# One layer pair on one core: a gate moved ahead, table terms written straight to DRAM, a norm split 320/192 with ScalarE's root

## The chip, the cores and the metric

The kernel runs on one core of a Trainium2 chip. The metric is the device time of one execution in microseconds; the number that counts is the median of the runs. Engines are named as the profile names them: PE (TensorE matmuls), PEld (its weight loads), DVE (VectorE), ACT (ScalarE), POOL (GpSimd), SP (the queue that issues DMAs).

## The reference

512 tokens of width 1024 go through two blocks. The first is a convolution and a dilated attention side by side, then a feed-forward part; the second is a hybrid layer:

```python
proj = h @ w_in                                   # h: rms norm of x, modulated
xa, za, q, k, v, zb, qi, ki, wi, ga, gb = jnp.split(proj, IN_SPLITS, axis=-1)
ya = jax.nn.gelu(s5_mixer(xa, a_re, a_im, b_re, b_im, c_re, c_im, d_skip, log_dt))
g = ya @ w_glu + b_glu
ya = g[..., :SSM_WIDTH] * jax.nn.sigmoid(g[..., SSM_WIDTH:])
ya = (ya * jax.nn.silu(za)) @ w_a_o
yb = dsa_mixer(q, k, v, qi, ki, wi)               # attention over selected keys
yb = (yb * jax.nn.silu(zb)) @ w_b_o
merged = jax.nn.sigmoid(ga) * ya + jax.nn.sigmoid(gb) * yb
x = x + gate * (merged @ w_out)
return rms_norm_2(x, final_g)                     # x * rsqrt(mean(x*x) + 1e-6) * g
```

In the first block `mix = concat(rms_norm(y_conv), rms_norm(y_attn))` and `x + mix @ w_out`.

## The kernel before

Everything is held with channels on the 128 partitions and tokens (512) along the free axis. A product with a weight matrix runs in blocks of 128 output channels; weights and operands are split into a high and a low part (`wh`, `wl` and `hh`, `hl` and the like), so each block takes three matmuls for each 128 input channels: 24 matmuls for 1024, all into one accumulator (`steps`, L193 to L195). A weight tile comes in by DMA (`raw`, three buffers), ACT casts it to `wh` (L97) and DVE subtracts `wl` (L98).

The order on PE is made by interleaving: attention is written as the main line, and a generator (`self.filler`) is stepped between its parts to put projection matmuls in its gaps. `high_priority` lets the scheduler draw an instruction forward.

- **mix_out** (L544) multiplies the normed output of the convolution, later of the attention, by its half of `w_out`, eight columns of 128 outputs. Each column runs four input blocks. The sum of squares `sq` is turned into the root `r` behind column 0, and spread over the partitions by matmuls (`spread`) behind column 2. In the convolution the fourth input block (`ch`, `cl`, L504) is finished last.
- **ssm_tables** (L821 on) builds, between the gate and up products of the feed-forward part, three tables in DRAM (`tabs`) for the state space part: `tabs[0]` (`bts`, by PE transposes L933 and the ACT copy L934), `tabs[1]` (direct terms `kk`, PE L940, copied by ACT L943 and put into a block-triangular tile `tt` that POOL has cleared, by eight small DMAs inside the core, L954, and then one DMA to DRAM, L955) and `tabs[2]` (`ca`). `tt` and `bts` share one buffer (tag "io"). It is a generator, stepped between the feed-forward units. `nr` is a tile of its own.
- **gates** (L1237) is the filler of the second block's attention: eight projections for `szb` and `sza`, then eight gate projections with Tanh (`tanhs`), and the four output chunks of the state space part (`chunk_out`, L1194). A chunk copies the states `hs` (POOL), loads `cat` and `tt` from `tabs` (L1202, L1204) and runs eight pairs of matmuls (L1208, L1209). `cat` and `tt` of all chunks share two buffers, so a chunk's loads are issued when the chunk before has read both. Six gates come first, then chunk 0, gate 6, chunk 1, gate 7, chunk 2, chunk 3.
- **The last norm**: output blocks 5 to 7 of the last product run as two halves of 256 tokens, all three of the first half (`last(n, 0)`) and then those of the second. `norm(e)` sums the squares of a half by ones matmuls (L1383, L1386), takes the diagonal (L225, L228), makes the root by integer guess and three Newton steps on DVE (`rsqrt`, L204 to L212), spreads it (L236), and DVE multiplies the eight blocks (L1397), with an output DMA for each two. The first half's norm is interleaved with `last(6, 1)` and `last(7, 1)`.
- **WARM** fp32 matmuls on a tile of ones (L67) run at the start.

## Time and profile before

| | |
|---|---|
| median of three runs | 1020.39 us (1019.31 to 1023.40) |
| the profiled execution | 1019.43 us |
| its span in the trace | 1017.6 us (1.8 us lie around it) |
| mean granted clock of PE | 0.994 |
| PE busy | 992.5 us, 98% |
| DVE, ACT, POOL busy | 687.6, 420.7, 145.2 us |
| DMA moved | 125.12 MB, mean 123 GB/s |

Times in the rows are from the start of the span. PE's share is an average over all stages; a matmul's duration includes its way through the array, so what one costs in a stream is read from start to start. An idle time in brackets, with an arrow, names what the engine waited for last.

### The profile page before, as it was taken

To read this page: it belongs to the slowest core of one execution; us is meant where nothing else is said; L and a number is where in the kernel's file an instruction comes from. 1 tells how busy PE (TensorE), PEld (TensorE's weight loads), DVE (VectorE), ACT (ScalarE), POOL (GpSimd) and SP (SyncE) were. 2 spreads that over 40 slices of the span, in tenths; PEclk is the share of its full clock that TensorE was granted. 3 is DMA by queue.
4 is the path that set the end of the run, shared out by engine and by line. 5 is a ranking of instruction groups with operands and counts; after the bars stand their busy time and mean duration, and the time that the engine had idled before them with its cause. 6 is when DMAs were issued, how large, how long until landed. Compare 5 with 4: busy or idle time off the path is not lost.

```text
span 1017.6 us, 13862 instructions
## 1 busy us (share of the span) xinstructions
PE 992.5 (98%) x5074; PEld 824.4 (81%) x5074; DVE 687.6 (68%) x1334; ACT 420.7 (41%) x710; POOL 145.2 (14%) x324
## 2 busy tenths in 40 slices
PE   9999999999999999999999999999999979999995
PEld 7888887887777778888888898788888878888885
DVE  6886778786997847787653238599995555544444
ACT  6455556443333333233222225556445553333251
POOL 0000000007711100000010100001888130000020
PEclk9999999999999999999999999999999999999998
DMA  7343221223245576465552323343222352343212
GB/s 268 98 135 104 79 84 42 63 89 127 67 142 171 142 219 213 144 203 185 169 170 90 114 93 129 121 133 112 89 83 104 109 160 63 116 173 104 83 42 83
DMA packets 56100, 125.12 MB, mean 123 GB/s; under 512 B 17824, under 2 KB 24480, under 8 KB 55904
## 3 DMA queue, kind: packets, MB, share of 16 engines
q1 hardware_dynamic: 55888, 124.19, 37.6%
q8 instruction: 40, 0.66, 0.3%
q14 instruction: 28, 0.23, 0.1%
q10 hardware_dynamic: 144, 0.05, 0.0%
HBM read 110.45 MB, written 12.58 MB: 121 GB/s over the span
## 4 chain that ended last, share of the span: by engine, by line
PE 89%; DVE 3%; DMA 3%; POOL 3%; issue 1%; SPq 1%; ACT 0%; DVEq 0%; ACTq 0%; POOLq 0%
PE acc L193 24%; PE acc L195 23%; PE acc L194 23%; PE acc L376 2%; PE acc L374 2%; PE acc L375 2%; PE acc L283 2%; PE tp L306 2%; PE sc L255 1%; PE sc L254 1%; DVE wl L98 1%; POOL stt L751 1%; PE acc L1209 1%; PE acc L1152 1%; PE acc L1208 1%
## 5 line engine op out<-in xcount | busy, mean ns | idle before, releaser
L97 ACT CAST wh<-raw 128x1024 fp32r<-128x1024 f32 x156 | 161.6, 1037 | 300.0 <-PE acc L194 245.9
L98 DVE TENSOR_TENSOR wl<-raw,wh 128x1024 fp32r<-128x1024 f32 x156 | 188.8, 1211 | 92.8 <-ACT wh L97 91.3
L193 PE MATMUL acc<-fh,wh 128*128 128x512 f32 x336 | 133.1, 396 | 2.2 <-DVE gs L617 2.2
L195 PE MATMUL acc<-fh,wl 128*128 128x512 f32 x336 | 131.1, 390 | 0.0
L194 PE MATMUL acc<-fl,wh 128*128 128x512 f32 x336 | 131.0, 390 | 0.0
L193 PE MATMUL acc<-hh,wh 128*128 128x512 f32 (+1 forms) x280 | 111.7, 399 | 0.0
L195 PE MATMUL acc<-hh,wl 128*128 128x512 f32 (+1 forms) x280 | 109.6, 391 | 0.0
L194 PE MATMUL acc<-hl,wh 128*128 128x512 f32 (+1 forms) x280 | 109.4, 391 | 0.0
L193 PEld LDWEIGHTS acc<-fh,wh 128*128 128x128 f32 x336 | 63.1, 188 | 17.1 <-DVE gs L617 2.6
L195 PEld LDWEIGHTS acc<-fh,wl 128*128 128x128 f32 x336 | 63.1, 188 | 13.3
L193 PE MATMUL acc<-th,wh 128*128 128x512 f32 (+1 forms) x198 | 73.7, 372 | 0.0
L194 PEld LDWEIGHTS acc<-fl,wh 128*128 128x128 f32 x336 | 63.2, 188 | 12.9 <-issue 0.2
L195 PE MATMUL acc<-th,wl 128*128 128x512 f32 (+1 forms) x198 | 73.4, 371 | 0.0
L194 PE MATMUL acc<-tl,wh 128*128 128x512 f32 (+1 forms) x198 | 73.4, 371 | 0.0
L195 PEld LDWEIGHTS acc<-hh,wl 128*128 128x128 f32 (+1 forms) x280 | 52.2, 186 | 12.1
L262 ACT ACTIVATE e<-z,mn 128x128 f32<-128x128 f32 (+3 forms) x64 | 36.1, 564 | 61.0 <-DVE mn L258 60.8
L193 PEld LDWEIGHTS acc<-hh,wh 128*128 128x128 f32 (+1 forms) x280 | 52.3, 187 | 10.5 <-issue 1.2
L194 PEld LDWEIGHTS acc<-hl,wh 128*128 128x128 f32 (+1 forms) x280 | 52.3, 187 | 9.6
L1162 POOL TENSOR_TENSOR hm<-H,a 128x64 f32<-128x64 f32 x63 | 28.0, 444 | 116.0 <-ACT H L1156 111.1
L193 PEld LDWEIGHTS acc<-th,wh 128*128 128x128 f32 x198 | 37.3, 189 | 7.1
L194 PEld LDWEIGHTS acc<-tl,wh 128*128 128x128 f32 x198 | 37.3, 188 | 7.1
L195 PEld LDWEIGHTS acc<-th,wl 128*128 128x128 f32 x198 | 37.3, 188 | 7.0
(400 smaller groups left out, 2080.6 us busy)
## 6 DMA issues: line engine op xcount, KB each, us to landing
raw<-in_wgu SPq DMA_DIRECT2D x44, 512.0 KB, 3.6
raw<-in_win SPq DMA_DIRECT2D x37, 512.0 KB, 3.5
mraw<-in_wmod SPq DMA_DIRECT2D x24, 512.0 KB, 4.6
raw<-in_wout SPq DMA_DIRECT2D x16, 512.0 KB, 3.5
raw<-in_wdown SPq DMA_DIRECT2D x16, 512.0 KB, 3.5
raw<-in_wconv SPq DMA_DIRECT2D x12, 512.0 KB, 3.5
raw<-in_wqkv SPq DMA_DIRECT2D x10, 512.0 KB, 4.2
x<-in_xT SPq DMA_DIRECT2D x16, 256.0 KB, 5.0
```

Source lines behind the costliest of these rows:

```text
L97: self.A.copy(hi, raw)
L98: self.V.tensor_sub(lo, raw, hi.bitcast(F))
L193: self.T.matmul(out, lh, rh, start=start, stop=False)
L194: self.T.matmul(out, lh, rl, start=False, stop=False)
L195: self.T.matmul(out, ll, rh, start=False, stop=stop)
L262: self.A.activation(e[:, :n], z[:, :n], AF.Exp, bias=mn, scale=-1.0, accum_out=den)
L283: self.T.matmul(self.yp[64 * e:64 * e + 64, pr * P:(pr + 1) * P], value(j, 2 * pr + e), pTs[u - h0 + 2 * pr + e][:, j * P:(j + 1) * P], st ...
L306: self.T.transpose(pp[:, j * P:(j + 1) * P], e[:, j * P:(j + 1) * P], self.ident)
L374: T.matmul(ps[i], xh[k][:, t], wh[:, kk], start=k == 0, stop=False)
L375: T.matmul(ps[i], xh[k][:, t], wl[:, kk], start=False, stop=False)
L376: T.matmul(ps[i], xl[k][:, t], wh[:, kk], start=False, stop=k == 7)
L1162: G.tensor_mul(m, H[:, c - 1, None].to_broadcast([P, 2, 2, 16]), self.a8.rearrange("p (w r) g -> p w r g", w=2))
```

## The change

1. `WARM` goes from 8 to 10.
2. `mix_out` runs the first three input blocks of columns 0 and 1, then the fourth of each; the root is taken behind the first (attention) or second (convolution) of these three-quarter columns.
3. `nr` is written to one of the two `gs` buffers of the feed-forward part ("lent").
4. The direct terms `kk` are written by their eight DMAs straight to `tabs[1]` in DRAM; the tile `tt`, its clearing and its DMA are gone; the part that must be zero is written by one DMA per chunk from a small tile `zt`. `bts` has a buffer of its own. One more `yield` per chunk.
5. Five gates come first, then chunk 0, gate 5, chunk 1, gate 6, chunk 2, gate 7, chunk 3.
6. The last norm takes tokens 0 to 319 and 320 to 511. Root: ScalarE's Sqrt, DVE's reciprocal and one Newton step, on 64 partitions; spread and diagonal in blocks of 64 tokens (5 and 3). A Sqrt on one column (`one`) stands ahead of the last product. `last(7, 1)` makes three steps instead of two before the first norm's end.

```diff
--- before.py
+++ after.py
@@ -27,7 +27,7 @@
 NT1 = 13
 KS = 3
 RAW = 3
-WARM = 8
+WARM = 10
 FILLA = (3.0, 4.0, 5.0, 2.6)
 FILLE = (5.5, 4.5, 3.5, 4.0)
 
@@ -219,13 +219,28 @@
             self.T.matmul(p, self.ones, sq, start=m == 0, stop=m == len(sqs) - 1)
         return self.rms_of(pool, p, n, tag, room)
 
-    def rms_of(self, pool, p, n, tag, room=None):
+    def root(self, pool, s, scale, eps):
+
+        sh = list(s.shape)
+        v, t, y = (pool.tile(sh, F, name="root" + c) for c in "vty")
+        V = self.V
+        V.tensor_scalar(v, s, scale, eps, op0=OP.mult, op1=OP.add)
+        self.A.activation(t, v, AF.Sqrt)
+        V.reciprocal(y, t)
+        V.scalar_tensor_tensor(v, v, -0.5, y, op0=OP.mult, op1=OP.mult)
+        V.tensor_mul(t, v, y)
+        V.scalar_tensor_tensor(y, t, 1.5, y, op0=OP.add, op1=OP.mult)
+        return y
+
+    def rms_of(self, pool, p, n, tag, room=None, root=False):
         toks = p.shape[1] // P
         d = pool.tile([P, 4, P], F, name="spd")[:, :toks]
         self.V.tensor_mul(d, p.rearrange("p (i t) -> p i t", t=P),
                           self.ident[:, None, :].to_broadcast([P, toks, P]))
         s = pool.tile([P, 4], F, name=tag + "s")[:, :toks]
         self.V.tensor_reduce(s, d, axis=AX.X, op=OP.add)
+        if root:
+            return self.root(pool, s, 1.0 / n, EPS)
         return self.rsqrt(pool, s, 1.0 / n, EPS, tag, room)
 
     def spread(self, pool, r, out=None):
@@ -539,20 +554,31 @@
             square(3)
             for _ in range(3):
                 yield
-            yield from mix_out(ch, sqc)
-
-        def mix_out(ys, sq):
+            yield from mix_out(ch, sqc, 1)
+
+        def mix_out(ys, sq, late):
 
             pend = []
             for n in range(8):
                 if n % 2 == 0:
                     wh, wl = self.w()
-                p = self.acc()
                 cs = slice(n % 2 * P, n % 2 * P + P)
-                yield from self.steps(p, (wh[:, :, cs], wl[:, :, cs]), ys)
+                if n == 0:
+                    p, p1 = self.acc(), self.acc()
+                    c1 = slice(P, 2 * P)
+                    for e, (q, c) in enumerate(((p, cs), (p1, c1))):
+                        yield from self.steps(q, (wh[:, :, c], wl[:, :, c]), ys, range(3))
+                        if e == late:
+                            with self.tc.high_priority(offset=LEAD):
+                                r = self.rms(sm, [sq], 512, "rx")
+                    yield from self.steps(p, (wh[:, :, cs], wl[:, :, cs]), ys, range(3, 4))
+                elif n == 1:
+                    p = p1
+                    yield from self.steps(p, (wh[:, :, cs], wl[:, :, cs]), ys, range(3, 4))
+                else:
+                    p = self.acc()
+                    yield from self.steps(p, (wh[:, :, cs], wl[:, :, cs]), ys)
                 with self.tc.high_priority(offset=LEAD):
-                    if n == 0:
-                        r = self.rms(sm, [sq], 512, "rx")
                     if n == 2:
                         Rn = self.spread(sm, r, sm.tile([P, S], F, name="Rx"))
                 pend.append((n, p))
@@ -576,7 +602,7 @@
             V.scalar_tensor_tensor(lo, y[:, j], g, hi.bitcast(F), op0=OP.mult, op1=OP.subtract)
             yh.append((hi, lo))
         self.drain()
-        self.run(mix_out(yh, sqa))
+        self.run(mix_out(yh, sqa, 0))
         cst.close()
         st.close()
         return x1
@@ -594,7 +620,7 @@
         tpool = self.pool(tq, "tF")
         ts = [(tpool.tile([P, S], R, name=f"th{j}"), tpool.tile([P, S], R, name=f"tl{j}")) for j in range(NT1)]
         tabs = ExitStack()
-        table = self.ssm_tables(tabs)
+        table = self.ssm_tables(tabs, lambda: wg.tile([P, S], F, name="gs", bufs=2)[:, :48])
         for _ in range(2):
             next(table)
         xs = []
@@ -818,7 +844,8 @@
             out.append(p)
         return out
 
-    def ssm_tables(self, st):
+    def ssm_tables(self, st, room):
+
         nc, a, V, A, G, T = self.nc, self.a, self.V, self.A, self.G, self.T
         p = self.pool(st, "tables")
         yield
@@ -872,7 +899,7 @@
         rden = p.tile([P, 48], F, name="srd")
         V.reciprocal(rden, den)
         yield
-        nr = p.tile([P, 48], F, name="snr")
+        nr = room()
         V.tensor_scalar(nr, pr[:, 1], -1.0, None, op0=OP.add)
         cr = p.tile([P, 48], F, name="scr")
         ci = p.tile([P, 48], F, name="sci")
@@ -903,6 +930,8 @@
         V.tensor_scalar(bc[:, 2], bc[:, 2], sg, None, op0=OP.mult)
         yield
         self.tabs = self.dram.tile([3, 4, P, S * 2], F, name="tabs")
+        zt = p.tile([P, 112], F, name="zt")
+        G.memset(zt, 0.0)
         for c in range(4):
             gs = slice(8 * c, 8 * c + 8)
             def table(x, y, nj, name):
@@ -924,7 +953,10 @@
             ca = yield from table(bc[:, 2], bc[:, 3], 9, "ca")
             nc.sync.dma_start(self.tabs[2, c].rearrange("p (g x) -> p g x", g=8),
                                 ca[:, :, 1:].rearrange("p g j x -> p g (j x)"))
-            bts = p.tile([P, 8, P], F, name="bts", tag="io")
+            yield
+            tt = self.tabs[1, c].rearrange("p (g x) -> p g x", g=8)
+            nc.sync.dma_start(tt[0:112, :, 0:112], zt[0:112, None].to_broadcast([112, 8, 112]))
+            bts = p.tile([P, 8, P], F, name="bts")
             kk = p.tile([16, 8, P], F, name="kk")
             for h in range(2):
                 yield
@@ -947,12 +979,9 @@
             V.tensor_mul(de, self.ident[0:16, None, 0:16].to_broadcast([16, 8, 16]),
                          dsk[:, gs, None].to_broadcast([16, 8, 16]))
             V.tensor_add(kk[:, :, 0:16], kk[:, :, 0:16], de)
-            tt = p.tile([P, 8, P], F, name="tt", tag="io")
-            G.memset(tt, 0.0)
             for j in range(8):
                 s = 7 - j
                 nc.sync.dma_start(tt[16 * j:16 * j + 16, :, 16 * s:], kk[:, :, 0:P - 16 * s])
-            nc.sync.dma_start(self.tabs[1, c], tt.rearrange("p g x -> p (g x)"))
 
 
     def mod_start(self):
@@ -1244,14 +1273,14 @@
                 for j in js:
                     A.activation(thb[j], (yield from self.proj(xs)), AF.Tanh, scale=0.5)
 
-            yield from tanhs(range(6))
+            yield from tanhs(range(5))
             for _ in cin:
                 pass
             s1.close()
             sso = self.pool(ss, "ssmout", side="right")
             for c in range(4):
                 yield from chunk_out(sso, c)
-                yield from tanhs(range(6 + c, min(7 + c, 8)))
+                yield from tanhs(range(5 + c, min(6 + c, 8)))
 
         sels = [sel, select(2), select(3)]
 
@@ -1346,6 +1375,8 @@
                 V.scalar_tensor_tensor(lo, m1[n], 0.5, hi.bitcast(F), op0=OP.mult, op1=OP.subtract)
                 mg.append((hi, lo))
         sq = x3p.tile([P, S], F, name="sqE")
+        one = x3p.tile([P, 1], F, name="one")
+        A.activation(one, self.ones[:, 0:1], AF.Sqrt)
         ws = [self.w() for _ in range(2)]
         ps = [self.acc() for _ in range(2)]
         for ks in (range(6), range(6, 8)):
@@ -1362,6 +1393,7 @@
                 G.tensor_add(sq, sq, s2)
         ws = [self.w() for _ in range(3)]
         ps = [self.acc() for _ in range(3)]
+        t0, t1 = slice(0, 320), slice(320, S)
         sqs = [[sq[:, t0]], [sq[:, t1]]]
 
         def last(n, e):
@@ -1376,22 +1408,33 @@
             sqs[e].append(s2)
 
         def norm(e):
+
             t = (t0, t1)[e]
-            p = self.tp()[:, :S // 2]
+            n = t.stop - t.start
+            b = n // 64
+            p = self.tp()[:, :n]
             with self.tc.high_priority(offset=200):
                 for m in range(3):
                     T.matmul(p, self.ones, sqs[e][m], start=m == 0, stop=False)
             yield
             with self.tc.high_priority(offset=200):
                 T.matmul(p, self.ones, sqs[e][3], start=False, stop=True)
-                r = self.rms_of(x3p, p, D, "re")
+                d = x3p.tile([64, 5, 64], F, name="spd")[:, :b]
+                V.tensor_mul(d, p[0:64].rearrange("p (i t) -> p i t", t=64),
+                             self.ident[0:64, None, 0:64].to_broadcast([64, b, 64]))
+                r = x3p.tile([64, 5], F, name="res")[:, :b]
+                V.tensor_reduce(r, d, axis=AX.X, op=OP.add)
+                r = self.root(x3p, r, 1.0 / D, EPS)
             for k in range(8):
                 A.activation(x3[k][:, t], x3[k][:, t], AF.Copy, scale=self.col("final_g_2", k))
             yield
             with self.tc.high_priority(offset=200):
-                Rl = self.spread(x3p, r)
+                Rl = self.tp()[:, :n]
+                for i in range(b):
+                    T.matmul(Rl[:, i * 64:(i + 1) * 64], r[:, i:i + 1].to_broadcast([64, P]), self.ident[0:64, 0:64],
+                             start=True, stop=True)
             if e == 0:
-                Rs = x3p.tile([P, S // 2], F, name="Rs")
+                Rs = x3p.tile([P, 320], F, name="Rs")
                 A.copy(Rs, Rl)
             for k in range(8):
                 V.tensor_mul(x3[k][:, t], x3[k][:, t], Rl if e else Rs)
@@ -1402,13 +1445,13 @@
         for n in range(5, 8):
             self.run(last(n, 0))
         self.run(last(5, 1))
-        self.pad(x3p, 352)
+        self.pad(x3p, 320)
         first, second = norm(0), norm(1)
         next(first)
         next(first)
         self.run(last(6, 1))
         b = last(7, 1)
-        for _ in range(2):
+        for _ in range(3):
             next(b)
         self.run(first)
         for _ in range(2):
```

On PE, from the end of chunk 2 to the first matmuls of chunk 3 (`hs,cat` and `U,tt` are a chunk's pairs; `ident,e` are attention transposes; `pT,vt` its value products; the trace shows two pieces for each fp32 matmul). Before:

```order
L1208 MATMUL acc<-hs,cat 128x64
L1209 MATMUL acc<-U,tt 128x64
L1208 MATMUL acc<-hs,cat 128x64
L1209 MATMUL acc<-U,tt 128x64
L283 MATMUL acc<-pT,vt 64x128 x16
L1208 MATMUL acc<-hs,cat 128x64
L1209 MATMUL acc<-U,tt 128x64
```

and with the change:

```order
L1237 MATMUL acc<-hs,cat 128x64
L1238 MATMUL acc<-U,tt 128x64
L193 MATMUL acc<-hh_4616,wh 128x512
L194 MATMUL acc<-hl_4617,wh 128x512
L195 MATMUL acc<-hh_4616,wl 128x512
L321 MATMUL tp<-ident,e 128x128 x8
L193 MATMUL acc<-hh_4618,wh 128x512
...
L193 MATMUL acc<-hh_4630,wh 128x512
L194 MATMUL acc<-hl_4631,wh 128x512
L195 MATMUL acc<-hh_4630,wl 128x512
L1237 MATMUL acc<-hs,cat 128x64
L1238 MATMUL acc<-U,tt 128x64
L298 MATMUL acc<-pT,vt 64x128 x16
```

Eight projection steps (24 matmuls) and eight transposes now stand between the two chunks.

On DVE, the last norm's first part (`x` L1373/L1405 is the residual step of an output block, L1397/L1440 the multiplications by the root). Before:

```order
L225 TENSOR_TENSOR spd<-tp,ident 128x256
L228 TENSOR_REDUCE res<-spd 128x2
L204 TENSOR_SCALAR rev<-res 128x2
L205 TENSOR_SCALAR rey<-rev 128x2
...
L209 TENSOR_TENSOR ret<-rev,rey 128x2
L1373 SCALAR_TENSOR_TENSOR x_8638<-acc,mod,x_8638 128x256
L210 SCALAR_TENSOR_TENSOR rey<-ret,rey 128x2
...
L210 SCALAR_TENSOR_TENSOR rey<-ret,rey 128x2
L1397 TENSOR_TENSOR x_8638<-x_8638,Rs 128x256 x8
L1373 SCALAR_TENSOR_TENSOR x_8638<-acc,mod,x_8638 128x256
L225 TENSOR_TENSOR spd<-tp,ident 128x256
```

and with the change:

```order
L1423 TENSOR_TENSOR spd<-tp,ident 64x320
L1426 TENSOR_REDUCE res<-spd 64x5
L227 TENSOR_SCALAR rootv<-res 64x5
L229 RECIPROCAL rooty<-roott 64x5
L230 SCALAR_TENSOR_TENSOR rootv<-rootv,rooty 64x5
L231 TENSOR_TENSOR roott<-rootv,rooty 64x5
L232 SCALAR_TENSOR_TENSOR rooty<-roott,rooty 64x5
L1405 SCALAR_TENSOR_TENSOR x_8634<-acc,mod,x_8634 128x192
L1440 TENSOR_TENSOR x_8634<-x_8634,Rs 128x320 x8
L1405 SCALAR_TENSOR_TENSOR x_8634<-acc,mod,x_8634 128x192
L1423 TENSOR_TENSOR spd<-tp,ident 64x192
```

The integer guess and the Newton steps are gone; the last `x` step stands behind the first part's eight multiplications in both, which are 320 columns wide now.

On ACT, around the last product, with the change (`th` is a gate's Tanh, `s` a square, `roott` the root); before, the only table load is the one at the start of the program:

```order
L1379 ACT_TABLE_LOAD
L1379 ACTIVATE one<-ones 128x1
L1344 ACTIVATE yah_8625<-th 128x512
L97 CAST wh<-raw 128x1024
L1366 ACT_TABLE_LOAD
L1366 ACTIVATE th<-acc 128x512
...
L1407 ACTIVATE s_9374<-x_8634 128x192
L1429 ACTIVATE x_8634<-x_8634,cols 128x192
L228 ACT_TABLE_LOAD
L228 ACTIVATE roott<-rootv 64x5
L1407 ACTIVATE s_9429<-x_8634 128x192
```

The Sqrt of `one` stands ahead of Tanhs, and a third load stands at the root.

## Rows read from the trace of the kernel before

**Rows 1.** The page's first section: busy time, share and instructions of each engine

```profile
PE 992.5 (98%) x5074; PEld 824.4 (81%) x5074; DVE 687.6 (68%) x1334; ACT 420.7 (41%) x710; POOL 145.2 (14%) x324
```

**Rows 2.** PE's waits: line, releaser, us in total, times, longest

```profile
PE acc L1208 <- DMA cat<-tabs: 5.5, 1, 5.5
...
PE acc L193 <- DVE gs L617: 2.2, 1, 2.2
PE tp L933 <- ACT bts L934: 1.7, 1, 1.7
...
PE acc L194 <- DVE cl L504: 0.8, 1, 0.8
...
PE tp L940 <- DVE ca L920: 0.5, 1, 0.5
```

**Rows 3.** The tile `cat`: its four loads from issue to landing

```profile
DMA to landing us min/median/max: 3.5/4.3/5.5
```

**Rows 4.** Timeline of PE, 800 to 850 us: start, duration, instruction

```profile
801.57 0.33 PE L1208 MATMUL acc<-hs,cat 128*128 128x64 f32 x2
...
822.61 1.97 PE L283 MATMUL acc<-pT,vt 128*64 128x128 f32 x32
...
829.79 1.04 PE L306 MATMUL tp<-ident,e 128*128 128x128 f32 x8
830.67 0.34 PE L1208 MATMUL acc<-hs,cat 128*128 128x64 f32 x2
...
833.52 0.39 PE L1209 MATMUL acc<-U,tt 128*128 128x64 f32 x2
...
840.50 0.69 PE L1209 MATMUL acc<-U,tt 128*128 128x64 f32 x2 [0.46 <-DMA tt<-tabs]
841.12 3.50 PE L283 MATMUL acc<-pT,vt 128*64 128x128 f32 x32
```

**Rows 5.** Busy time by engine, 842 to 844 us; PEclk is the granted clock

```profile
842.00:844.00 2.00, 2.00 (x24) 2.00 (x22) 0.00 (x0) 0.00 (x0) 0.00 (x0) 0.50 0.25 56
```

**Rows 6.** Timeline of POOL, 776 to 792 us

```profile
786.13 3.78 POOL L1199 COPY hs<-H 64x252 f32<-64x252 f32 x4
```

**Rows 7.** Timeline of ACT, 315 to 324 us

```profile
321.84 0.58 ACT L934 COPY bts<-tp 128x512 f32<-128x512 f32 x1 [5.32 <-DMA tabs<-tt]
```

**Rows 8.** Busy PE, PEld, DVE, ACT, POOL, clock, DMA share, GB/s, 280 to 306

```profile
280.00:306.00 26.00, 25.54 (x127) 20.30 (x126) 25.90 (x32) 9.42 (x16) 4.38 (x3) 1.00 0.47 148
```

**Rows 9.** Timeline of PE, 983 to 988 us: 512 and then 256 columns

```profile
983.63 0.39 PE L193 MATMUL acc<-mh,wh 128*128 128x512 f32 x1
...
984.31 0.28 PE L193 MATMUL acc<-mh,wh 128*128 128x256 f32 x1
...
987.18 0.28 PE L193 MATMUL acc<-mh,wh 128*128 128x256 f32 x1
```

**Rows 10.** Timeline of the end, all engines, 1001 to 1018 us

```profile
1001.70 0.71 PE L236 MATMUL tp<-ident,rey 128*128 128x128 f32 x4 [0.39 <-DVE rey L210]
...
1002.85 2.78 DVE L1397 TENSOR_TENSOR x<-x,Rs 128x256 f32<-128x256 f32 x8 [1.21 <-ACT Rs L1395]
...
1005.88 0.48 DVE L1373 SCALAR_TENSOR_TENSOR x<-acc,mod,x 128x256 f32<-128x256 f32 x1 [0.26 <-PE acc L195]
...
1008.52 0.17 DVE L204 TENSOR_SCALAR rev<-res 128x2 f32<-128x2 f32 x1
...
1010.75 0.68 PE L236 MATMUL tp<-ident,rey 128*128 128x128 f32 x4 [3.19 <-DVE rey L210]
1011.47 2.74 DVE L1397 TENSOR_TENSOR x<-x,tp 128x256 f32<-128x256 f32 x8 [0.86 <-PE tp L236]
```

**Rows 11.** Timeline of ACT, 0 to 6 us

```profile
1.17 1.28 ACT L64 ACT_TABLE_LOAD   x1 [1.17 <-PEq L1507]
2.46 0.20 ACT L64 ACTIVATE warm<-ones 128x1 f32<-128x1 f32 x1
```

## The prediction

> **What bounds the kernel now.** I read the page first: PE is busy for 992.5 us, 98% of the span [rows 1]. In such a kernel an edit pays only if it removes matmul time, fills a hole in which PE waits, or shortens what follows the last matmul. The next view is therefore the list of PE's own waits [rows 2]; the reader is to see that one hole of 5.5 us is as long as the others shown there together, and that each has one releaser. Then the timeline around that hole [rows 4], with what PE does when it comes back. Last the end of the program [rows 10], where no matmul hides anything. DVE's 68% and ScalarE's 41% of the span say nothing here: what counts is who is late at each hole.
>
> **Gates, the large term.** In the before kernel chunks 2 and 3 of `chunk_out` stand back to back. Both table buffers are in use until chunk 2's last matmul (833.52), so `cat` of chunk 3 is issued only then, and PE waits 5.47 us for it and 0.46 us for `tt` [rows 2, 4]. Loads of this kind take 3.5 to 5.5 us to land [rows 3]. With `range(5)` the projection of gate 7 stands between these chunks: 24 matmuls and 8 transposes. A 512-column matmul takes 0.227 us from start to start (983.63 to 984.31, three of them [rows 9]), a transpose 0.11 (829.79 to 830.67, eight of them [rows 4]): 24 x 0.227 + 8 x 0.11 = 6.3 us, longer than the 5.5 us of the slowest `cat`. The wait of 5.93 us goes. What is late next is `tt`, which now ends 7 us after chunk 2 (840.50 against 833.52): in the worst case 0.5 us stays.
>
> There is a second loss at the same place, which the waits don't list. In the stretch behind the hole the granted clock is 0.50, the lower of the two levels (1.2 GHz), while PE is busy all the time [rows 5]. The 32 value matmuls there span 3.50 us; the same 32 behind chunk 1 span 1.97 [rows 4]: 1.53 us. The `tt` pair at 840.50 spans 0.69 us and a pair at full clock 0.39 (833.52 [rows 4]): 0.30. Before the clock fell PE had stood still for 5.47 us. If the hole is filled the drop has no cause, so 1.83 us go with it. **Gates: -7.76 us**, between -7.3 and -7.8.
>
> The price: chunk 0 comes 24 matmuls and 8 small ones earlier, 6.3 to 8.3 us by the same rows. Its `hs` is copied by POOL until 786.13 + 3.78 = 789.91, and PE now starts it at 801.57 [rows 4, 6]; 801.6 - 8.3 = 793.3, so 3.4 us of room stay. I cost it at nothing. Chunks 0 and 1 keep one projection each between them and their successors, as now.
>
> **mix_out.** PE waits 0.8 us for the last `cl` of the convolution [rows 2]. Three quarters of two columns now stand ahead of the first matmul that reads it, 9 x 0.227 = 2.0 us more work [rows 9], so the wait goes: **-0.77**, bounds 0 and -0.8. The root of the squares starts later by less than that and the multiplication with `Rx` has room.
>
> **Direct terms and the lent buffer.** The wait of 1.7 us at L933 ends with ScalarE's `bts` copy, which itself had waited 5.32 us for the transfer of the `tt` tile that shared its buffer [rows 2, 7]. The change gives `bts` a buffer of its own and drops that tile, its four clears and four transfers: **-1.67**, at best also the 0.5 of L940 right behind, at worst nothing if DVE's table work is late there anyway. Added are four transfers of zeros, 0.4 MB each, ahead of the weight loads. In the DMA-rich stretch shown, a share of 0.47 moved 148 GB/s [rows 8]; at that rate 1.6 MB take 11 us, at the full share 5. Weights are loaded three ahead, and each 512 KB feed about 24 matmuls, 5.4 us, so 16 us of work stand in front: nothing. The clear of `zt` and the lent `nr` stand in DVE's and POOL's order where nobody waits for them. The 2.2 us hole at `gs` [rows 2] stays, since what stands ahead of it on DVE and POOL is not touched. Two more warm-up matmuls end before the first operand is there: nothing, within 0.2.
>
> **The last norm.** The split into 320 and 192 columns costs PE time. 24 matmuls of 256 columns take 2.87 us (984.31 to 987.18), 0.120 each, and 512 columns 0.227 [rows 9]; between these 320 take 0.147. For 192 there is no row. If a matmul were only its columns, 0.093 would come out by the same line. But the transposes with fresh weights and 128 columns take 0.11 each, where that line gives 0.067 [rows 4]: something other than columns sets a floor, and I take 0.113 for 192. Three output blocks per part, 72 matmuls each: 72 x (0.147 + 0.113) - 144 x 0.120 = +1.4 us; by columns alone 0; with 0.120, the nearest row above, +1.9.
>
> On this the Trainium skill speaks against the change: "TensorE: Matmul & The Clock Gate", section "LDWEIGHTS (loading the stationary operand)", gives a load of 128 weight columns as 128/1.2, some 107 ns whatever is streamed; by an estimate from it 192 columns would cost at least 0.107 us, and the term above would be +1.0 instead of 0. The transposes agree with that floor (0.11); no run here shows 192 columns.
>
> The remaining pieces, from the end rows. The first part's spread now needs 10 small matmul pieces for the present 4 (0.71 us, 1001.70 [rows 10]), at 0.11 each +0.40; the 0.39 us for which it waited go, since the root needs five short steps on DVE and one on ScalarE for twelve. DVE then multiplies eight blocks of 320 columns: 2.78 us at 256 (1002.85 [rows 10]) become about 3.22. PE's remaining 15 matmuls shrink to 192 columns, so the last `x` step, which had met a free DVE (0.26 us idle at 1005.88), stands behind these multiplications: from the spread on, PE needs 3.8 us, DVE 4.9, so **+0.9**. The tail behind it: now 8.33 us from 1005.88 to 1014.21. Of it 2.64 lie ahead of the root (192 columns: 2.35), 2.23 from the root's start to the spread (1008.52 to 1010.75; five DVE steps of 0.2 and one ScalarE step with two hand-overs: 1.4), 0.72 for the spread (six pieces: 0.95) and 2.74 for eight multiplications (192 columns: 2.15) [rows 10]. Sum 6.85, so -1.47. **Last norm: +1.4 + 0.4 - 0.4 + 0.9 - 1.5 = +0.8 us**, with 192 columns by their columns alone -0.3, at most +2.
>
> ScalarE's root needs another function table. The preload `one` is in vain: in the new order a Tanh follows it, and a third table load stands right ahead of the first root. A load took 1.28 us and the next activation started at once [rows 11]. It can start when ScalarE's last copy ends, about when PE closes the sum; DVE's two reductions run beside it for 1.0 us, and in the new order PE has 33 more matmuls, 33 x 0.113 = 3.7 us, ahead of the spread, while the root is there some 2.7 us after the sum (0.9 for the two reductions, 1.3 for the load or what runs beside it, the short steps behind). Hidden, with 1 us to spare.
>
> "ScalarE: Activation LUTs", section "What ACT_TABLE_LOAD costs", of the Trainium skill counts 2.66 us for each switch, a drain of 1.38 us with it. The row shows no such pause at the start of the program; with it the first root would come 1 us later, still about when PE gets there, and the sum would rise by 0 to 0.3.
>
> **Sum**: -7.76 - 0.77 - 1.67 + 0.8 = -9.4 us on the profiled run of 1019.43, so 1010.0. The median of the three runs is 0.96 above the profiled run; I put half of it on top: **1010.5**.
>
> **Rivals.** (a) *192 columns go by their columns*: 1.1 less, 1009.4. For it: 256 and 512 lie on one line; against: the transposes. (b) *The table stage opens new waits.* DVE is busy for 25.9 of 26 us there [rows 8], and the change reorders the table's steps among the evacuations of the gates and adds a pause per chunk. One wait as long as that at `gs` (2.2 us [rows 2]) gives 1012.7, two 1014.9. Against: from chunk 1 on only two holes stand there now, and one of them was the shared buffer's. (c) *The same, at every transposition group*: eight L933 groups of the table each wait 2.2 us behind DVE: +17.6, 1028, slower than before. It decides from the fifth wait on, which eats the gain. (d) *The clock or part of the wait stays*: if `tt` still ends late and more loads share the queues, PE waits up to 2 us and, should it lose the clock again, 1.8 more: 1014.3. (e) *The new root does not do what it says*: the table load lands on the path, +1.3 and a drain's worth more: 1012 to 1013.
>
> **How the numbers follow.** Forecast within 1.5 us of 1010.5: 0.55. (a) 0.13. (b) 0.15, a third of it from two waits up. (c) 0.04. (d) 0.06. (e) 0.07. The range: below, (a) with all bounds at their best, 1007.5; above, two waits with the last norm at +2, 1016. A measurement of this kernel tells 0.5%, 5.1 us, from no change: faster is under 1015.3, slower over 1025.5. Forecast, (a), (e), most of (d) and of (b) are faster: 0.87. The rest of (b) and (d): same, 0.09. (c): slower, 0.04.
>
> **What would show it.** Gates: no wait of L1208's successor over 0.6 us, and 32 value matmuls behind the first pair of chunk 3 in about 2 us at a clock of 1.00. mix_out: no PE wait for `cl`. Direct terms: ScalarE's `bts` waits for PE, not for a transfer. Last norm: start to start 0.113 us in the 192-column blocks (0.093 would be (a)), the last `x` step waiting for DVE's own multiplications, a table load in front of the first root and no PE wait at its spread. The forecast is wrong if PE's waits at the table's lines sum to over 3 us, if chunk 0 waits for `hs`, or if the tail behind the last `x` isn't shorter by 1 us.

## The result and the profile after

The changed kernel takes 1012.61 us in the median of five runs (1011.92 to 1015.11); before it was 1020.39. The ratio is 0.992, with a 95% interval of 0.990 to 0.995. On a second occasion it was 0.993 (0.991 to 0.994). The profiled execution has a span of 1010.1 us for 1017.6, 7.5 us less. The forecast was 1010.5 within 1007.5 to 1016, and faster. The range and the direction held; the median lies 2.1 us above the forecast, outside the 1.5 us around it that had the chance of 0.55. Three of the terms were off, in opposite directions, so that part of their errors cancelled.

PE's waits after the change, which answer to [rows 2]:

```profile
PE acc L193 <- DVE gs L643: 2.2, 1, 2.2
PE tp L1434 <- DVE rooty L232: 2.1, 1, 2.1
PE tp L1421 <- ACT s L1407: 1.7, 1, 1.7
PE tp L251 <- DVE rxy L210: 1.4, 1, 1.4
PE tp L67 <- POOL ones L62: 1.0, 1, 1.0
PE tp L321 <- DVE e L280: 1.0, 1, 1.0
```

The wait for `cat`, the one for `cl` and both at the table's transpositions are gone. Two are new: before the spread of the convolution's root (`rxy`, 1.4) and before an attention transpose (`e`, 1.0). Both stand in the stage that mix_out changes.

The place that carried the large term, timeline of PE (start, duration, instruction), to be set against [rows 4]:

```profile
826.31 0.39 PE L1238 MATMUL acc<-U,tt 128*128 128x64 f32 x2
...
832.95 0.33 PE L1237 MATMUL acc<-hs,cat 128*128 128x64 f32 x2
833.41 0.43 PE L1238 MATMUL acc<-U,tt 128*128 128x64 f32 x2
833.78 1.97 PE L298 MATMUL acc<-pT,vt 128*64 128x128 f32 x32
```

Chunk 3 starts 6.6 us after chunk 2's last pair, with matmuls all the way, and the 32 value pieces take 1.97 us for 3.50. The busy time of the engines in 836 to 840 us, where PE had been busy for 0.62 of the 4 us before, shows it busy throughout and a granted clock of 1.00 (the third last number):

```profile
836.00:840.00 4.00, 4.00 (x32) 3.82 (x32) 3.26 (x10) 2.18 (x4) 0.00 (x0) 1.00 0.32 86
```

To see where the 7.5 us lie, I took the start of the same PE instruction in both traces:

| PE instruction | before | after | difference |
|---|---|---|---|
| first operand matmul of the program | 5.43 | 5.35 | -0.1 |
| spread of the convolution's root | 179.38 | 180.93 | +1.6 |
| spread of the feed-forward root | 252.97 | 254.61 | +1.6 |
| a feed-forward matmul behind the tables | 375.91 | 374.90 | -1.0 |
| last scores matmul ahead of chunk 0 and gate 5 (`sc<-kl,q`) | 792.65 | 791.79 | -0.9 |
| value piece behind chunk 3's first pair | 844.16 | 835.36 | -8.8 |
| end of the span | 1017.6 | 1010.1 | -7.5 |

So by stages: mix_out +1.6, tables -2.6, gates -7.9, last norm +1.3, and 0.2 more between them.

### The profile page after: what moved, and what is told of

Read it like the earlier page. It is cut to its first block, busy times and chain, and to the rows that moved or that the text cites. A ratio compares the mean times of both kernels' runs of the same rounds, so it can differ in the third digit from the quotient of the medians.

```text
span 1010.1 us, 13859 instructions
## 1 busy us (share of the span) xinstructions
PE 993.6 (98%) x5086; PEld 825.7 (82%) x5086; DVE 683.1 (68%) x1320; ACT 426.1 (42%) x716; POOL 137.5 (14%) x321
## 4 chain that ended last, share of the span: by engine, by line
PE 92%; DVE 2%; POOL 2%; DMA 1%; issue 1%; ACT 1%; SPq 0%; DVEq 0%; POOLq 0%
PE acc L193 25%; PE acc L195 24%; PE acc L194 24%; PE acc L389 2%; PE acc L390 2%; PE acc L391 2%; PE acc L298 2%; PE tp L321 2%; PE sc L270 1%; PE sc L269 1%; POOL stt L777 1%; DMA sg<-in_sgn 1%; PE acc L1238 1%; PE acc L1237 1%; PE acc L1181 1%
## 5 line engine op out<-in xcount | busy, mean ns | idle before, releaser
L193 PEld LDWEIGHTS acc<-fh,wh 128*128 128x128 f32 x336 | 63.1, 188 | 17.2 <-DVE gs L643 2.6
```

The costliest lines, as they stand in the source:

```text
L193: self.T.matmul(out, lh, rh, start=start, stop=False)
```

## The experiments

All medians are given as ratios to the kernel before, which ran beside each of them.

### One part at a time

Gates alone:

```diff
-            yield from tanhs(range(6))
+            yield from tanhs(range(5))
...
-                yield from tanhs(range(6 + c, min(7 + c, 8)))
+                yield from tanhs(range(5 + c, min(6 + c, 8)))
```

> The kernel before with only the gates moved (five, then chunk 0, gate 5, and so on). Theory: PE's wait of 5.93 us before chunk 3 goes and with it the half clock behind it (1.83 us): 7.5 us less, about 1012.8, and 32 value pieces in 2.0 us. Rival: only the wait is saved and the clock falls anyway: 5.9 us less, about 1014.5.

Measured: 0.991 (0.989 to 0.993), 1012.7 us for 1021.2. The 32 value pieces behind chunk 3's first pair:

```profile
835.45 1.97 PE L283 MATMUL acc<-pT,vt 128*64 128x128 f32 x32
```

Wait and half clock (a granted clock of 0.50) go together; the rival is out. The median fell by 8.5 us. In the traces PE's way from the last scores matmul ahead of chunk 0 to these value pieces is 8.3 us shorter here; in the full change it was 7.9, because `tt` came a little late there.

mix_out alone: the two hunks of the diff in `mix_out` and its calls, nothing else.

> The kernel before with only mix_out's two three-quarter columns. Theory: the 0.77 us hole before the fourth block is filled, but PE then stands before the softmax result e (about 1 us) and before the spread of the root (about 1.4 us), since the sum of squares now comes about 4 us later: 1.6 us more, about 1022. Rival (the loss in the changed kernel came from the other parts): 0.8 us less, about 1019.6.

Measured: 1.001 (0.999 to 1.002), 0.2 us more in the median, with an interval from 0.7 us less to 2.1 more. The median does not separate the two. The trace does; PE's timeline with the idle time in brackets:

```profile
170.85 0.63 PE L306 MATMUL tp<-ident,e 128*128 128x128 f32 x4 [0.96 <-DVE e L265]
...
182.52 1.13 PE L236 MATMUL tp<-ident,rxy 128*128 128x128 f32 x8 [1.43 <-DVE rxy L210]
```

The same two waits within a hundredth, without any other part of the change. They belong to mix_out.

Direct terms, own buffer and lent `nr` alone (the hunks in `ffn` and `ssm_tables`):

> The kernel before with only the direct terms, the own buffer for bts and the lent nr. Theory: no PE wait at the two transposition lines of the tables and 2.1 to 2.6 us less, about 1018. Rival of the prediction: only the 1.67 us wait goes, about 1018.7, or new waits of 2.2 us each appear there.

Measured: 1.000 (0.998 to 1.001), from 2.1 us less to 1.3 more. No PE wait at the table's transpositions is left in its trace, and in the table stage PE gains 2.6 us on the kernel before, as with the full change. It had lost as much ahead of that: 1.0 us by a longer wait for the feed-forward root (1.3 us for 0.5), which is taken up below, and 1.6 right behind the `gs` hole, where the granted clock had fallen to 0.50. The loss behind `gs` is not the change's own (see the last section), but it bears on what the change is worth. The run of mix_out alone had the same loss with the old tables, and there the two table waits were 0.3 us in all for the 2.1 of the kernel before:

```profile
PE tp L944 <- ACT bts L945: 0.3, 1, 0.3
```

In that one profile the old tables made good most of what the clock had cost; without the wait nothing does. So the median can gain less than the 2.6 us.

The last norm alone:

> The kernel before with only the last norm changed (320 and 192 tokens, ScalarE's root). Theory: 192 columns cost 0.111 us a matmul, the last residual step waits for DVE's eight wide multiplications, and the last spread runs at half clock: 1.2 us more, about 1021.6. Rival (192 columns by their columns alone, 0.093): 0.3 us less.

Measured: 1.000 (0.999 to 1.002), from 1.4 us less to 1.6 more: the median can't place an effect of this size. Its trace shows the same two waits at the end as the full change (1.75 and 2.11 us), and from the first matmul of the last product to the end it takes 1.5 us more than the kernel before.

### Undoing mix_out, and its order apart

The changed kernel was run again beside these as a reference:

> The changed kernel again, so that the next three can be set against it on one chip. 7.5 to 8.5 us less than before.

Measured: 0.993 (0.991 to 0.994), 1014.5 us.

The changed kernel with the `mix_out` of before (those two hunks taken back):

> The changed kernel with the mix_out of before. Theory (the later root costs 1.43 us at the spread and the filled hole comes back at the softmax): the 0.77 us hole returns, both new waits go, 1.6 us less than the changed kernel. Rival (mix_out is neutral, as its run alone in the median suggests): no difference over 0.5 us.

Measured: 0.990 (0.988 to 0.992), 1010.7 us, 3.8 less than the changed kernel beside it. The direction is the theory's, the size over twice what its trace can give. In the two profiles, which both lost clock behind `gs`, PE reaches the spread 1.4 us earlier, loses 0.3 of that at the feed-forward root and 0.5 at the end, where the clock falls sooner, and the program ends 0.6 earlier. The rival, no difference over 0.5 us, is out for the stage; the rest of the 3.8 us I can't place.

The changed kernel with the sum of squares behind the first three-quarter column:

```diff
-            yield from mix_out(ch, sqc, 1)
+            yield from mix_out(ch, sqc, 0)
```

> The changed kernel, but in the convolution too the sum of squares is taken behind the first three-quarter column. Theory: the root is early again and the 1.43 us wait at the spread goes; PE instead waits about 1.5 us for the sum of squares itself, so within 0.7 us of the changed kernel. Rival: filling the hole pays once the root is early: 1.5 to 2 us less than the changed kernel.

Measured: 0.991 (0.989 to 0.992), 1012.3 us, 2.3 less than the changed kernel. In its trace PE stands still for the sum of squares itself, and the spread no longer waits:

```profile
168.12 2.07 PE L219 MATMUL tp<-sqc,ones 128*128 128x512 f32 x2 [2.00 <-DVE sqc L528]
...
182.12 1.05 PE L251 MATMUL tp<-ident,rxy 128*128 128x128 f32 x8
```

Both new waits (2.4 us) have become one of 2.00, where before one of 0.77 stood. But the granted clock is 0.50 behind it:

```profile
169.00:170.00 1.00, 1.00 (x3) 0.35 (x2) 0.05 (x1) 0.00 (x0) 0.00 (x0) 0.50 0.00 0
```

The spread comes at 182.12, later than before (179.38) and than in the changed kernel (180.93). The stage is thus 2.6 us longer than before, and 1.1 longer than in the changed kernel: more than the 0.7 that the theory allowed, because it had the wait and not the clock. That the run is faster all the same is not this stage's doing: in the two profiles it ends 0.9 us earlier, and the changed kernel's had lost 1.5 us by the clock behind `gs`, which this one kept, and waited 1.3 us for the feed-forward root where this one waited 0.8. In the traces neither order of the split beats the order of before.

### The last norm in halves

As the run with the old mix_out, and:

```diff
-        t0, t1 = slice(0, 320), slice(320, S)
+        t0, t1 = slice(0, S // 2), slice(S // 2, S)
...
-                Rs = x3p.tile([P, 320], F, name="Rs")
+                Rs = x3p.tile([P, S // 2], F, name="Rs")
...
-        for _ in range(3):
+        for _ in range(2):
             next(b)
```

> As the run with the old mix_out, and the last norm in two halves of 256 with ScalarE's root. Theory (192 columns at 0.111 us, so the split costs PE 1.3 us, and DVE's wide multiplications hold the last residual step): PE's part is 1.3 us shorter, the wait of the last residual step is under 0.4 us, the tail behind it 0.7 us longer (wider steps, less the half clock): 1.0 us less than the run with the old mix_out. Rival (the smaller second part pays in the tail): 0.5 us more.

Measured: 0.989 (0.987 to 0.991), 1010.0 us, 0.7 less than the run with the old mix_out; the intervals overlap, so the sign is the theory's but not shown by the median alone. Its trace bears the mechanism out in two of three points: 256 columns at 0.120 us, and a last `x` step that starts as soon as PE ends. The third did not come: the last spread runs at half clock here too.

This trace also showed what the direct terms cost. Timeline of POOL, at the copy that opens the table's work:

```profile
238.28 0.82 POOL L933 COPY ca<-bc 128x128 f32<-128x128 f32 x1 [1.82 <-DVE bc L919]
```

POOL waits for DVE's step on `bc`, and that for the landing of `bc` (237.40) and of the small load `sg` issued behind it (237.57). The queue of that time:

```profile
228.14 0.42 SPq L844 DMA_DIRECT2D bc<-in_ssm_bc  x1
...
229.56 8.77 SPq L947 DMA_DIRECT2D tabs<-zt  x4
```

The four transfers of zeros are issued right behind `bc`. Behind POOL's copy stands the chain that ends in the feed-forward root's DVE steps, and PE waits 1.55 us there:

```profile
PE tp L251 <- DVE rfy L210: 1.6, 1, 1.6
```

### The zeros later, the table of before, the clock at the end, the warm-up

As the run in halves, with the zeros made from a tile that comes later, so that their transfers are issued some 55 us later (284.6 for 229.6):

```diff
-        G.memset(zt, 0.0)
+        A.activation(zt, bx[:, 0:7].rearrange("p g x -> p (g x)"), AF.Copy, scale=0.0)
```

> As the run with the old mix_out and halves, but the zeros are made from bx, so that their four transfers come about 40 us later. Theory (the zeros' transfers share the queues with bc, POOL's chain of the decay table then waits for bc and PE for the root rfy): POOL's chain from tab to sx falls from 18.4 to about 17.0 us, PE's wait at rfy from 1.55 to about 0.5: 1.0 us less. Rival (POOL's chain varies by itself): 17 to 18.4 us again and no difference.

Measured: 0.990 (0.988 to 0.991), 1010.8 us. From its issue to its landing `bc` took 8.1 us, in the run before 9.3:

```profile
bc<-in_ssm_bc SPq DMA_DIRECT2D x1, 1024.0 KB, 8.1
```

```profile
bc<-in_ssm_bc SPq DMA_DIRECT2D x1, 1024.0 KB, 9.3
```

POOL's chain, counted from its first step (`ex_c`) to DVE's step `sx` behind it, took 17.2 us for 18.4, and PE's wait fell from 1.55 to 0.51:

```profile
237.97 0.81 POOL L933 COPY ca<-bc 128x128 f32<-128x128 f32 x1 [0.53 <-issue]
```

```profile
PE tp L251 <- DVE rfy L210: 0.5, 1, 0.5
```

POOL's chain over all profiles: 16.7 to 17.1 us in the four with the tables as before, 17.2 to 18.4 in the six with the zeros behind `bc` (17.2 in the profile shown of the changed kernel, 18.0 in its second one), 17.2 in the four in which they come later or not at all. `bc` landed 8.2 to 9.3 us after its issue in the six, 6.6 to 8.2 in the eight others. So the traces show the mechanism in five of the six profiles that have it, by 0.4 to 1.2 us of POOL's chain; the forecast 1 us is not seen in the medians.

The table of before, with only a buffer of its own for `bts` (old mix_out, halves, no zeros):

```diff
-            bts = p.tile([P, 8, P], F, name="bts", tag="io")
+            bts = p.tile([P, 8, P], F, name="bts")
```

> As the run with the old mix_out and halves, but without the direct terms: the table of before with its tile, its clearing and its transfer, and only a buffer of its own for bts. Theory (the wait at the table's transpositions came from the shared buffer alone): no PE wait there, and no zeros ahead of bc, so 0.5 to 1.2 us less than the run with the direct terms. Rival (writing straight to DRAM saves something itself): 0.5 us or more longer.

Measured: 0.989 (0.987 to 0.991), 1010.5 us, in its ratio the same as with the direct terms; neither the 0.5 to 1.2 us less of the theory nor the 0.5 more of the rival can be told from the medians. Its trace has no PE wait at the transpositions and 0.50 us at the feed-forward root, and PE gains the same 2.6 us in the table stage. The separate buffer is the whole of that gain; writing straight to DRAM adds nothing that these runs can tell.

Six matmuls on a spare accumulator around the last sum of squares, on top of the later zeros; their results are not used:

```diff
+            dm = self.acc()[:, :n] if e else None
+            def busy(m):
+                for _ in range(m):
+                    T.matmul(dm, self.ones, sq[:, t], start=True, stop=True)
+            if e:
+                busy(2)
...
                 T.matmul(p, self.ones, sqs[e][3], start=False, stop=True)
+                if e:
+                    busy(4)
```

> As the run before in this list, with six more fp32 matmuls on a spare accumulator around the last sum of squares; their results are not used. Theory (PE's two idle times at the end cost half the clock in the last spread): the granted clock stays 1.00 there, the last spread's eight pieces take about 1.0 us for 2.0: 0.6 to 1.0 us less. Rival (the added matmuls delay the last sum or the spread): 0.3 us or more longer.

Measured: 0.988 (0.986 to 0.990), 1008.4 us, the best of all, for 1010.8 without them (the intervals overlap). The last spread of the two kernels, first without the added matmuls:

```profile
1001.88 1.93 PE L1423 MATMUL tp<-ident,rooty 64*128 64x64 f32 x8 [2.25 <-DVE rooty L232]
```

and with them:

```profile
999.67 1.07 PE L1431 MATMUL tp<-ident,rooty 64*128 64x64 f32 x8 [0.52 <-DVE rooty L232]
```

The granted clock during these spreads is 0.50 and 1.00. From the last `x` step to the last multiplications it is 5.04 us for 5.90. So the half clock at the end costs 0.9 us in the traces, and matmuls that nobody needs buy it back. The rest of the 2.4 us between the medians is not theirs: the profile without them had also lost 1.6 us by the clock behind `gs`, the one with them had not.

Eight warm-up matmuls for ten, otherwise as the run with the later zeros:

```diff
-WARM = 10
+WARM = 8
```

> As the first of this list with eight warm-up matmuls instead of ten. Theory of the prediction: no difference, within 0.2 us. Rival (the two more close the hole in front of the first operands, and without them the clock can fall at the start): up to 1.7 us more, with a stretch at 0.50 between 5 and 12 us in the profile.

Measured: 0.989 (0.987 to 0.991), 1010.3 us for 1010.8 with ten: no difference in the median. But the profile shows what the rival spoke of, the first matmuls at half pace (0.43 us from start to start for 0.227):

```profile
6.39 0.63 PE L391 MATMUL acc<-wh,xl 128*128 128x512 f32 x1
6.82 0.63 PE L389 MATMUL acc<-wh,xh 128*128 128x512 f32 x1
```

This lasts some ten matmuls and costs 1.6 to 1.9 us where it comes. It stands in three of the six profiles with eight warm-up matmuls (the gates alone, mix_out alone and this one) and in none of the eight with ten. So few profiles don't settle it, and the medians don't show it.

## Why the prediction was right, and where it was wrong

**Gates: right.** -7.76 was forecast, -7.9 is in the traces. Both halves of the term were needed: the 5.93 us of waiting and the 1.83 us of half clock behind it, which no list of waits shows. One piece of the half clock was left out: the first `cat` pair behind the hole, with 0.66 us for the 0.33 of a pair at full clock:

```profile
839.38 0.66 PE L1208 MATMUL acc<-hs,cat 128*128 128x64 f32 x2 [5.47 <-DMA cat<-tabs]
```

Against it stands what is left of the `tt` wait: in the changed kernel that pair starts 0.46 us after its `cat` pair (832.95 to 833.41) and not 0.17 (829.40 to 829.57 before). Chunk 0 did not wait for `hs`.

**mix_out: wrong, and it is the largest miss.** Forecast -0.77, found +1.6. The hole before `cl` was filled as said. The step that failed is the sentence that the root "starts later by less than that and the multiplication with `Rx` has room". Before, PE's sum of squares and DVE's root stood like this:

```profile
168.07 1.10 PE L219 MATMUL tp<-sqc,ones 128*128 128x512 f32 x2
...
179.38 1.05 PE L236 MATMUL tp<-ident,rxy 128*128 128x128 f32 x8
```

and DVE's last step of the root at 173.10, so 6 us of room:

```profile
173.10 0.16 DVE L210 SCALAR_TENSOR_TENSOR rxy<-rxt,rxy 128x4 f32<-128x4 f32 x1
```

After, PE first and then DVE:

```profile
172.09 1.02 PE L219 MATMUL tp<-sqc,ones 128*128 128x512 f32 x2
...
180.93 1.13 PE L251 MATMUL tp<-ident,rxy 128*128 128x128 f32 x8 [1.43 <-DVE rxy L210]
```

```profile
173.68 0.68 DVE L238 TENSOR_TENSOR spd<-tp,ident 128x512 f32<-128x512 f32 x1
...
175.85 1.23 DVE L98 TENSOR_TENSOR wl<-raw,wh 128x1024 fp32r<-128x1024 f32 x1
...
180.62 0.16 DVE L210 SCALAR_TENSOR_TENSOR rxy<-rxt,rxy 128x4 f32<-128x4 f32 x1
```

Two things were not counted. Six matmuls of mix_out later in PE's order is 4.0 us later in time (172.09 for 168.07), because eight transposes, 24 value products and the wait for `e` stand among them. And the root's twelve short DVE steps, which ran in 5.2 us from the sum to the end, now fall among a weight split and the attention's softmax and take 8.7. The new wait for `e` shows the other half: in this stage attention's softmax on DVE sets the pace, so PE, sent ahead through one hole, stands 1 us later before the next.

**Direct terms: right in kind, the term too small, and a cost missed.** Forecast -1.67, at best 2.1; found -2.6 here and when alone. The separate buffer did it, not the direct writing. "Weights are loaded three ahead [...] so 16 us of work stand in front: nothing" looked at the wrong transfer: PE waits for no weights there, but `bc`, issued just ahead of the zeros, landed later and held POOL's chain and with it the feed-forward root, by 0 to 1.1 us from profile to profile. The Trainium skill has a line that bears on it: "DMA: Bandwidth & Descriptors", section "Specifications", asks for 512 B or more in a transfer's pieces and has smaller ones read, modify and write. The zeros go out in rows of 448 B; no run here had them in longer rows, so how much of the delay is the row length stays open.

**Last norm: the size was nearly right.** Forecast +0.8, found +1.3. Timeline of PE in 320 and 192 columns (from the first row to the second it is ten matmuls, from the third to the fourth 24):

```profile
976.60 0.31 PE L195 MATMUL acc<-mh,wl 128*128 128x320 f32 x1
...
978.06 0.31 PE L193 MATMUL acc<-mh,wh 128*128 128x320 f32 x1
```

```profile
991.13 0.27 PE L193 MATMUL acc<-mh,wh 128*128 128x192 f32 x1
...
993.81 0.27 PE L193 MATMUL acc<-mh,wh 128*128 128x192 f32 x1
```

0.146 and 0.112 us, forecast 0.147 and 0.113: 192 columns cost what a fresh set of weights costs, not what their columns would, and the split makes PE about 1.3 us longer (72 matmuls of each, against the 0.120 of [rows 9]); rival (a) is out. That agrees with the floor of 107 ns that the Trainium skill gives for 128 weight columns ("TensorE: Matmul & The Clock Gate", "LDWEIGHTS (loading the stationary operand)"). The end, all engines:

```profile
990.81 1.28 ACT L228 ACT_TABLE_LOAD   x1
...
992.05 0.17 DVE L227 TENSOR_SCALAR rootv<-res 64x5 f32<-64x5 f32 x1
992.25 0.21 ACT L228 ACTIVATE roott<-rootv 64x5 f32<-64x5 f32 x1 [0.16 <-DVE rootv L227]
...
994.58 1.32 PE L1434 MATMUL tp<-ident,rooty 64*128 64x64 f32 x10
...
996.39 3.30 DVE L1440 TENSOR_TENSOR x<-x,Rs 128x320 f32<-128x320 f32 x8 [2.30 <-ACT Rs L1438]
...
999.62 0.41 DVE L1405 SCALAR_TENSOR_TENSOR x<-acc,mod,x 128x192 f32<-128x192 f32 x1
...
1001.87 0.16 DVE L227 TENSOR_SCALAR rootv<-res 64x3 f32<-64x3 f32 x1
...
1003.18 1.51 PE L1434 MATMUL tp<-ident,rooty 64*128 64x64 f32 x6 [2.11 <-DVE rooty L232]
1004.73 2.20 DVE L1440 TENSOR_TENSOR x<-x,tp 128x192 f32<-128x192 f32 x8 [1.70 <-PE tp L1434]
```

The table load stands in front of the first root and is hidden: it ends at 992.09, ScalarE waits for `rootv` after that, and PE does not wait at the spread (994.58). The preload was in vain and rival (e) did not come. The last `x` step starts right behind DVE's eight wide multiplications, with no idle time, 0.9 us after PE had ended (998.73 by its last matmul): forecast 0.9. The tail from 999.62 to 1006.93 is 7.31 us for a forecast 6.85, and one term carries the difference: the last spread took 1.55 us to the multiplications, not 0.95. Its clock was 0.50:

```profile
1003.00:1004.00 1.00, 0.82 (x4) 0.85 (x5) 0.03 (x1) 0.00 (x0) 0.00 (x0) 0.50 0.00 0
```

So the step that failed here is the 0.95 us for six pieces, a price at full clock: PE stands still for 1.75 and 2.11 us ahead of them, and the clock that this costs was not counted. The kernel before stood still for as long (1.02 and 3.19 us), and its clock fell too, but only behind its last spread:

```profile
1010.00:1011.00 1.00, 0.24 (x2) 0.28 (x3) 0.54 (x4) 0.00 (x0) 0.00 (x0) 1.00 0.00 0
...
1012.00:1013.00 1.00, 0.00 (x0) 0.00 (x0) 1.00 (x4) 0.00 (x0) 0.00 (x0) 0.50 0.00 0
```

It is not the longer wait for the last sum that does it. The four runs in halves without added matmuls stand still for 1.0 and 2.2 us, and their last spread runs at 0.50 as well. What decides whether the clock falls ahead of the spread or behind it stays open; keeping PE at work there keeps it up.

**The warm-up**, priced at nothing, gave nothing in the traces of the two kernels (-0.1) and in the medians; whether it keeps an occasional 1.7 us away stays open.

**The sum.** -9.4 was forecast for the profiled run and -7.5 came: mix_out 2.4 worse, the norm 0.5 worse, the tables 1.0 better, the gates 0.2 better, 0.2 worse between the stages. The range held because it had room for two new waits of 2.2 us (rival (b)). Two came, 2.4 us in all, but in another stage than the rival had put them. The median is close to what rival (b) gives for one wait (1012.7), and that is chance: no new wait came at the tables. That the tables gave 1.0 us more than forecast, which kept the sum from being further off, is luck as well.

## What to carry to other kernels

A hole that PE passes through costs twice if the clock falls behind it; look at the granted clock in the stretch after each long wait before pricing its removal. When a reduction is moved by some rows in PE's order, count what else stands in these rows and what its chain of short DVE steps will then be mixed with: its duration is not a constant. A bulk write without any dependency is issued at once; ask which load was issued just ahead of it, for here that one landed up to 1.1 us later than in any run without the write, while PE waited for no weights, which are loaded early.

## What the runs showed of the hardware that was not expected

The same hole does or does not cost clock, from one execution to the next. Behind the wait for `gs`, 2.2 to 2.3 us in all fourteen profiles, the granted clock fell to 0.50 in seven. The changed kernel in its two profiles, 264 to 266 us, first the one shown above:

```profile
264.00:266.00 2.00, 2.00 (x10) 1.68 (x9) 1.97 (x4) 0.24 (x2) 1.84 (x4) 1.00 0.04 8
```

```profile
264.00:266.00 2.00, 1.84 (x4) 1.49 (x5) 2.00 (x5) 0.63 (x1) 1.69 (x7) 0.52 0.04 8
```

The rows count four PE instructions in these 2 us for ten, and in all 1.5 to 1.6 us are lost behind the hole in each of the seven. The five runs of the changed kernel differ by 3.2 us; this can be half of it, and it is one reason why parts of 1 to 2 us could be told from traces but not from medians.

The hole before chunk 3 lost the clock in all four profiles that have it, but not for the same time. In the kernel before it is back at 1.00 in 848 to 852 us; in the run of the direct terms alone it is not, and 4.4 us more are lost between chunk 3 and the last product:

```profile
848.00:852.00 4.00, 4.00 (x17) 3.81 (x18) 1.36 (x2) 2.03 (x3) 0.00 (x0) 0.50 0.00 0
```

So the gate that fills this hole can take away more than the profile of the kernel before shows. Of the executions of kernels with the hole that ran beside the experiments, 23 of 83 have a mean granted clock of 0.988 or less, and take 1021.5 to 1026.5 us; without the hole no execution is below 0.993. That the long half clock is behind all of these is not shown, as only one of them was profiled.

At the start of the program, where three profiles show their first ten matmuls 0.43 us apart instead of 0.227, the column of the granted clock reads 1.00 all the same: there the pace has to be read from the starts.

A table load on ScalarE took 1.28 us in the middle of the program as at its start, and the next activation followed within 0.01 us, or waited only for its data (0.16 us at the last norm).
